# Second block's mixers: block inverses and query rotations held in PSUM, the forget gates' logarithm issued behind the decays

## The chip, the cores and the metric

The kernel runs as one program on one core of a Trainium2 chip. A core has five engines with a queue of instructions each: TensorE (PE in the rows; PEld is its weight load), VectorE (DVE), ScalarE (ACT), GpSimd (POOL) and SyncE (SP), which here only issues DMAs. The metric is device time in microseconds of one execution.

## The reference

Two blocks of two layers each follow one another on one sequence of 256 tokens with 1024 channels, in float32. The change touches the mixers of the second block only. A mixer projects the normalised tokens into four groups, runs one mixer of width 256 on each, and projects the joined results back:

```python
for l in range(DEPTH):                                   # DEPTH = 2
    h = _rms_norm(x, norm1_g[l]) * (1.0 + sc1) + sh1
    pa, pb, pc, pd = _split(h @ w_in[l], GROUP_COLS)
    ya = _rwkv7_mixer(pa, ...)                           # A
    yb = _diff_attn_mixer(pb, ..., cos, sin, lambda_init)  # B
    yc = _spatial_gating_mixer(pc, ...)                  # C
    yd = _forgetting_attn_mixer(pd, ...)                 # D
    y = jnp.concatenate([ya, yb, yc, yd], axis=-1)
    x = x + g1 * (y @ w_out[l])
    h = _rms_norm(x, norm2_g[l]) * (1.0 + sc2) + sh2
    x = x + g2 * _conv_glu_ffn(h, ffn_up[l], ...)
```

Three pieces of it are worked differently after the change:

```python
def step(state, inp):                    # A: a recurrence over the tokens
    sa = einsum('bhvk,bhk->bhv', state, -kk_t)
    state = state * w_t + sa[..., None] * b_t + v_t[..., None] * k_t
    return state, einsum('bhvk,bhk->bhv', state, r_t)

q = _apply_rope(_rms_norm(q, q_g), cos, sin)             # B
k = _apply_rope(_rms_norm(k, k_g), cos, sin)

log_f = jax.nn.log_sigmoid(fl + f_b)                     # D
F = lax.cumsum(log_f, axis=2)
```

The kernel works A's recurrence by blocks of tokens, which needs inverses of triangular 32 x 32 blocks of a matrix of scores.

## The kernel before

The program runs eight stages after one another: GDN mixer, feed-forward, MLA mixer, feed-forward (first block), then mixer, feed-forward, mixer, feed-forward (second block). The second block's mixers lie at about 803 to 985 us and 1205 to 1385 us of the profiled span.

**Weights.** A weight chunk is loaded by SP's queue into `raw`, copied by ACT to a rounded `wh` (L464), and the residue `wl = raw - wh` is made on GpSimd (L467) or VectorE (L469), as a string in the plan says chunk by chunk. Each product takes three matmuls (`wh` with the high and the low part of the tokens, `wl` with the high part): L480 and L483 in one form, L492 to L494 in the other. Three `raw`, `wh` and `wl` buffers rotate.

**Order.** The plan gives the mixer an order string, `B V M b2+L D+S C / e s d c`: after A's scores (`rwkv_scores`) come the pieces of B, A's values (V), the forget gates (M), and so on; a `+` weaves two pieces. A scheduler turns this into one queue for each engine by priority, so an instruction that waits holds up what stands behind it on its engine. PSUM has four banks of tag "acc" for projections, two of tag "mm" and two of tag "A".

**A's scores** (`rwkv_scores`, mixer A). Low-rank inputs `a_P` go through Tanh (L1519, L1520) and a step on VectorE (L1521) to the matmuls `ps_lr` (L1551), which give the decays `a_lw` and the gates `a_av`. Running sums `a_cx` and their exponentials `a_eM`, `a_eK`, `a_eP` (L1571 to L1575) follow, then `a_BD` and `a_bt` on VectorE, and the scores `ps_sc` (L1597). These are copied to `a_UB`, written to DRAM (`dA`), and read back as 32 x 32 blocks into `a_AT` (SBUF, 128 partitions). `tri_inverse` starts from the identity T and makes 31 steps of two VectorE instructions each, a product into `a_stmp` (L1848) and a subtraction from T (L1849). Here T is part of `a_AT`. R, a copy of T, goes through DRAM again to `a_TR`, whose transposes are `ps_tr` (L1705). The first block's GDN mixer calls the same `tri_inverse` with T in a PSUM tile `psT`.

**B's heads** (`diff_heads`). The projection gives queries and keys of 128 tokens in one bank `ps_qk` (tag "acc"), 256 columns each; t = 0 and 1 are the two halves of the tokens. `head_norm` squares (ACT), sums (`hn_s`, VectorE), takes a reciprocal root, and multiplies `ps_qk` into the SBUF tile `b_xn` in one VectorE instruction (L1875), after which the bank is free. The rotation makes six instructions (L1914, L1915) for the queries on VectorE and six for the keys on GpSimd, all from SBUF to SBUF with `b_m` as scratch, into `b_ro`. Four transposes of `b_ro` follow on TensorE (L1925). The next projection, D's, is queued around them on TensorE and takes its banks in turn; `forget_heads` (D) uses `head_norm` too.

**D's gates** (`forget_gates`). With f the gates' input (`flog`, 4 x 256), VectorE makes -|f| (L2045), ACT Exp (L2046) and Ln (L2047) of it, VectorE joins them (L2048) and sums along the tokens (L2051). Exp and Ln need different tables of the scalar engine here, so an ACT_TABLE_LOAD stands ahead of Ln, and one ahead of the Tanh that follows.

The step of the inverse, and the rotation:

```python
V.tensor_tensor(tv, A[:, i, i+1:]..., T[:, i, :m]..., op=ALU.mult)                # L1848
V.tensor_tensor(T[:, i+1:, :m], T[:, i+1:, :m], tv, op=ALU.subtract)              # L1849
```

## Time and profile before

| | us |
|---|---|
| median of 3 runs | 1605.33 (1603.08 to 1606.51) |
| profiled execution | 1601.26 |
| its span | 1599.6 |
| TensorE busy | 1459.0 (91% of the span) |
| VectorE busy | 1148.4 (72%) |
| ScalarE busy | 816.5 (51%) |
| GpSimd busy | 658.3 (41%) |

The profile comes from one execution, 4.07 us below the median of the runs; 1.66 us of it lie outside the span. A share of busy time is an average over eight stages with different limits, so it has to be read stage by stage. A row of a timeline gives start, duration, engine, source line, operation and the tiles with their shapes; in brackets stands the idle time of the engine ahead of it and what ended that. Where a row says x2, x4, ... it joins so many instructions.

### The profile page before, as it was taken

What the parts mean: (1) busy time and instruction counts of PE and PEld (TensorE: products, weight loads), DVE (VectorE), ACT (ScalarE), POOL (GpSimd) and SP (SyncE); (2) the same over time, 40 slices, a digit from 0 to 9 for tenths busy, and PEclk for the clock granted to TensorE, in tenths of its full rate; (3) what the DMA queues carried; (4) which work ended last, traced back from release to release, by engine and by line L of the source; (5) the groups of instructions that cost most, each with busy time, mean ns of one, the idle gap of its engine ahead of it and who ended that gap; (6) DMA issues with size and microseconds to landing.
All of it is one profiled execution on the core that took longest, in us unless ns stands there. A gap on an engine that the chain in (4) does not pass through costs nothing. (4 is left out here: it accounts for less than half of the span.)

```text
span 1599.6 us, 25783 instructions
## 1 busy us (share of the span) xinstructions
PE 1459.0 (91%) x9586; PEld 1289.3 (81%) x9586; DVE 1148.4 (72%) x2348; ACT 816.5 (51%) x1479; POOL 658.3 (41%) x433
## 2 busy tenths in 40 slices
PE   5788989999999899999988889998998788899998
PEld 4788877789988788999877666898887666689987
DVE  4568677678677676997477696788966769676652
ACT  4765545444544564544354465555545446466651
POOL 4455632336443341443136422365534421336630
PEclk9899999999999999999999999999999999899999
DMA  4565531578785455887533324677663332365551
GB/s 161 170 175 173 158 100 57 170 263 305 279 303 184 144 189 187 329 319 298 174 112 116 116 66 134 251 269 265 256 240 127 115 103 67 106 240 184 190 192 40
DMA packets 103247, 292.96 MB, mean 183 GB/s; under 512 B 28073, under 2 KB 37969, under 8 KB 96977
## 3 DMA queue, kind: packets, MB, share of 16 engines
q1 hardware_dynamic: 93872, 237.12, 43.9%
q10 hardware_dynamic: 8896, 53.14, 9.0%
q8 instruction: 75, 1.23, 0.3%
q0 software_dynamic: 352, 1.06, 0.2%
q14 instruction: 52, 0.42, 0.1%
HBM read 288.04 MB, written 3.24 MB: 182 GB/s over the span
## 5 line engine op out<-in xcount | busy, mean ns | idle before, releaser
L467 POOL TENSOR_TENSOR wl<-raw,wh 128x1024 fp32r<-128x1024 f32 (+4 forms) x162 | 395.0, 2445 | 449.8 <-ACT wh L464 378.8
L464 ACT CAST wh<-raw 128x1024 fp32r<-128x1024 f32 (+3 forms) x421 | 422.9, 1018 | 249.6 <-PE ps_o L493 92.3
L469 DVE TENSOR_TENSOR wl<-raw,wh 128x1024 fp32r<-128x1024 f32 (+2 forms) x259 | 346.6, 1348 | 126.7 <-ACT wh L464 122.0
L480 PE MATMUL ps_gu<-h_hi,wh 128*128 128x256 f32 x1280 | 312.9, 283 | 7.3 <-DVE gu_u L2202 7.3
L480 PE MATMUL ps_gu<-h_lo,wh 128*128 128x256 f32 x1280 | 312.4, 283 | 0.0
L480 PEld LDWEIGHTS ps_gu<-h_hi,wh 128*128 128x128 f32 x1280 | 244.6, 191 | 8.2 <-issue 8.0
L480 PEld LDWEIGHTS ps_gu<-h_lo,wh 128*128 128x128 f32 x1280 | 244.7, 191 | 0.2
L1372 DVE CUSTOM_DVE_ANT_0 ada_raw<-ada_raw,ada_cond 128x1024 f32<-128x1024 f32 x96 | 176.2, 1851 | 53.5 <-DMA ada_raw<-in_ada 53.5
L483 PE MATMUL ps_gu<-h_hi,wl 128*128 128x256 f32 x1280 | 178.3, 282 | 4.0 <-POOL wl L467 3.6
L483 PEld LDWEIGHTS ps_gu<-h_hi,wl 128*128 128x128 f32 x1280 | 163.5, 191 | 4.6 <-POOL wl L467 4.0
L494 PE MATMUL ps_o<-wl,act_h 128*128 128x512 f32 x352 | 138.8, 394 | 0.0
L493 PE MATMUL ps_o<-wh,act_l 128*128 128x512 f32 x352 | 138.5, 394 | 0.0
L492 PE MATMUL ps_o<-wh,act_h 128*128 128x512 f32 x352 | 138.4, 393 | 0.0
L2202 DVE SCALAR_TENSOR_TENSOR gu_u<-ps_gu,f2s,gu_u 128x254 f32<-128x254 f32 (+1 forms) x176 | 81.4, 477 | 42.7 <-ACT gu_u L2200 38.8
L725 POOL TENSOR_TENSOR act_l<-gu_t,act_h 128x256 fp32r<-128x256 f32 x44 | 54.0, 1228 | 113.7 <-ACT act_h L724 111.8
L2205 POOL TENSOR_TENSOR gu_t<-gu_t,gu_u 128x256 f32<-128x256 f32 x44 | 49.9, 1134 | 85.0 <-DVE gu_u L2202 82.4
L494 PEld LDWEIGHTS ps_o<-wl,act_h 128*128 128x128 f32 x352 | 66.1, 188 | 15.4 <-issue 0.5
L493 PEld LDWEIGHTS ps_o<-wh,act_l 128*128 128x128 f32 x352 | 66.1, 188 | 15.0 <-issue 0.2
L492 PEld LDWEIGHTS ps_o<-wh,act_h 128*128 128x128 f32 x352 | 66.1, 188 | 15.0 <-issue 0.2
L740 DVE SCALAR_TENSOR_TENSOR cv_y<-ps_g,fi,cv_y 128x253 f32<-128x253 f32 (+2 forms) x96 | 45.0, 478 | 34.8 <-ACT cv_y L738 33.3
L480 PE MATMUL ps_g<-h_hi,wh 128*128 128x256 f32 x256 | 68.4, 300 | 0.0
L2206 ACT CAST act_h<-gu_t 128x256 fp32r<-128x256 f32 x44 | 17.9, 407 | 98.7 <-POOL gu_t L2205 98.5
(653 smaller groups left out, 3031.3 us busy)
## 6 DMA issues: line engine op xcount, KB each, us to landing
ada_raw<-in_ada ACTq DMA_DIRECT2D x48, 1024.0 KB, 5.8
raw<-in_f_gu SPq DMA_DIRECT2D x88, 512.0 KB, 4.5
raw<-in_u_gu SPq DMA_DIRECT2D x88, 512.0 KB, 4.3
raw<-in_f_dn SPq DMA_DIRECT2D x44, 512.0 KB, 4.2
raw<-in_u_dn SPq DMA_DIRECT2D x44, 512.0 KB, 3.7
raw<-in_g_qkv SPq DMA_DIRECT2D x32, 512.0 KB, 3.9
raw<-in_g_z SPq DMA_DIRECT2D x16, 512.0 KB, 4.7
raw<-in_g_out SPq DMA_DIRECT2D x16, 512.0 KB, 3.4
```

The costliest lines, as they stand in the source:

```text
L464: self.last_copy = nc.scalar.copy(wh[:, :cols], raw[:, :cols])
L467: nc.gpsimd.tensor_tensor(wl[:, :cols], raw[:, :cols], wh[:, :cols].bitcast(F32), op=ALU.subtract)
L469: nc.vector.tensor_tensor(wl[:, :cols], raw[:, :cols], wh[:, :cols].bitcast(F32), op=ALU.subtract)
L480: nc.tensor.matmul(ps, wh[:, k * width + m0 : k * width + m0 + m], xx[:, k, :], start=(n == 0), stop=(n == last))
L483: nc.tensor.matmul(ps, wl[:, k * width + m0 : k * width + m0 + m], xh[:, k, :], start=False, stop=(n == last))
L492: nc.tensor.matmul(ps, xh, wh[:, sl], start=start, stop=False, **kw)
L493: nc.tensor.matmul(ps, xl, wh[:, sl], start=False, stop=False, **kw)
L494: nc.tensor.matmul(ps, xh, wl[:, sl], start=False, stop=stop, **kw)
L725: nc.gpsimd.tensor_tensor(al[:, m, :], t, ah[:, m, :].bitcast(F32), op=ALU.subtract)
L1372: nc.vector.tensor_tensor_reduce(raw[:, j], raw[:, j], self.cond, 1.0, 0.0, op0=ALU.mult, op1=ALU.add, accum_out=mod[:, i : i + 1])
L2202: nc.vector.scalar_tensor_tensor(u[:, j, d:], ps[:, j, : S - d], cw[:, 3 * q + 2 - d : 3 * q + 3 - d], u[:, j, d:], op0=ALU.mult, op1=ALU.add)
L2205: nc.gpsimd.tensor_tensor(t, t, u[:, 0], op=ALU.mult)
```

## The change

Three parts, in both mixers of the second block:

- `rwkv_scores`: the matrix T of `tri_inverse` becomes a PSUM tile `ps_ti` of tag "A"; `a_AT` shrinks from 48 to 40 columns of 32. The first operands A and the scratch `a_stmp` stay in SBUF.
- `head_norm` becomes `head_scale`, which ends with the reciprocal root. In `diff_heads` the multiply is made in two halves: the keys from PSUM to `b_xn` (for GpSimd's rotation), the queries in place in `ps_qk`. The query rotation reads `ps_qk` and uses the keys' half of the bank as its scratch, so that each of its instructions has one operand in SBUF. `forget_heads` makes the multiply as before.
- `forget_gates`: Exp and Ln are issued behind the last of the exponentials `a_eP`.

```diff
@@ -1418,7 +1418,7 @@
             gate = self.gate_row(2, mp)
             A = self.rwkv_scores(l, hl, norm, mp, dr)
             B, C, Dd = {}, {}, {}
-            G = dict(B=lambda: self.diff_heads(l, hl, mp, B), C=lambda: self.spatial_in(l, hl, mp, C), D=lambda: self.forget_heads(l, hl, mp, Dd), M=lambda: self.forget_gates(mp, dr, A["f"], Dd),
+            G = dict(B=lambda: self.diff_heads(l, hl, mp, B), C=lambda: self.spatial_in(l, hl, mp, C), D=lambda: self.forget_heads(l, hl, mp, Dd), M=lambda: self.forget_gates(mp, dr, A["f"], Dd, A["last_exp"]),
                      V=lambda: self.rwkv_values(mp, A), L=lambda: self.rwkv_levels(mp, A), S=lambda: self.rwkv_scan(l, mp, A), s=lambda: self.rwkv_out(mp, A, yh, yl),
                      b=lambda: self.diff_attend(l, mp, B), e=lambda: self.diff_out(mp, B, yh, yl), c=lambda: self.spatial_out(l, mp, C, yh, yl), d=lambda: self.forget_attend(l, mp, Dd))
             yh = yl = None
@@ -1572,7 +1572,7 @@
         for m, n in mn:
             nc.scalar.activation(eK[:, m, n], cx[:, m, n, 0:128], AF.Exp, bias=ncm[:, m, n : n + 1])
         for m, n in mn:
-            nc.scalar.activation(eP[:, m, n], cx[:, m, n, 1:], AF.Exp, bias=ncm[:, m, n : n + 1])
+            last_exp = nc.scalar.activation(eP[:, m, n], cx[:, m, n, 1:], AF.Exp, bias=ncm[:, m, n : n + 1])
 
         k2 = t2("k2", [128, 2, S])
         for m in range(2):
@@ -1602,8 +1602,9 @@
             s32 = slice(32 * b, 32 * b + 32)
             nc.sync.dma_start(dA.rearrange("(q b) (j c) -> b j q c", b=4, c=32)[b], UB[s32, :, s32])
 
-        AT = mp.tile([128, 48, 32], F32, name="a_AT", tag="a_z2")
-        A, T, R = AT[:, 0:32], AT[:, 32:40].rearrange("p a b -> p (a b)").rearrange("p (c j) -> p c j", j=8), AT[:, 40:48]
+        AT = mp.tile([128, 40, 32], F32, name="a_AT", tag="a_z2")
+        A, R = AT[:, 0:32], AT[:, 32:40]
+        T = self.pm.tile([128, 32, 8], F32, name="ps_ti", tag="A")
         tmp = mp.tile([128, 256], F32, name="a_stmp", tag="a_y2", bufs=2)
         for g in range(4):
             (nc.sync, nc.scalar)[g % 2].dma_start(A[32 * g : 32 * g + 32].rearrange("p j c -> p (j c)"), dA)
@@ -1614,7 +1615,7 @@
         nc.gpsimd.affine_select(UB, UB, [[0, 8], [1, 128]], ALU.is_ge, 0.0, base=-1, channel_multiplier=-1)
         nc.gpsimd.affine_select(UB, UB, [[0, 8], [1, 128]], ALU.not_equal, 1.0, base=0, channel_multiplier=-1)
         a = locals()
-        a = {n: a[n] for n in "f UB dR BD bt kt k2 eP P7 lora esc kap S0 sel4".split()}
+        a = {n: a[n] for n in "f last_exp UB dR BD bt kt k2 eP P7 lora esc kap S0 sel4".split()}
         a["r"] = project("r", 0)
         a["v"] = project("v", 2)
         return a
@@ -1862,17 +1863,14 @@
             yield
         return ps, pv
 
-    def head_norm(self, mp, dst, ps, nh, hd, eps):
-
-        nc = self.nc
-        V = nc.vector
-        v = ps.rearrange("p (h d) -> p h d", h=nh)
-        nc.scalar.activation(dst, v, AF.Square)
+    def head_scale(self, junk, ps, nh, hd, eps):
+
+        self.nc.scalar.activation(junk, ps.rearrange("p (h d) -> p h d", h=nh), AF.Square)
         ss = self.sm.tile([128, nh], F32, name="hn_s", tag=f"hn_s{nh}")
-        V.tensor_reduce(ss, dst, axis=AX.X, op=ALU.add)
+        self.nc.vector.tensor_reduce(ss, junk, axis=AX.X, op=ALU.add)
         rs = self.sm.tile([128, nh], F32, name="hn_r", tag=f"hn_r{nh}")
         self.rsqrt(rs, ss, (128, nh), 1.0 / hd, eps)
-        V.tensor_tensor(dst, v, rs.unsqueeze(2).to_broadcast([128, nh, hd]), op=ALU.mult)
+        return rs
 
     def diff_heads(self, l, hl, mp, res):
         nc, ap = self.nc, self.ap
@@ -1904,21 +1902,23 @@
             if t == 0:
                 nc.scalar.copy(v, pv)
             xn = mp.tile([128, 16, 32], F32, name="b_xn", tag="b_xn", bufs=2)
-            self.head_norm(mp, xn, ps[t], 16, 32, 1e-6)
-            xv = xn.rearrange("p (q h) (s f) -> p q h s f", q=2, s=2)
+            rs = self.head_scale(xn, ps[t], 16, 32, 1e-6)
+            pv4 = ps[t].rearrange("p (q h d) -> p q h d", q=2, h=8)
+            xn4 = xn.rearrange("p (q h) d -> p q h d", q=2)
+            for q, dst in ((1, xn4[:, 1]), (0, pv4[:, 0])):
+                V.tensor_tensor(dst, pv4[:, q], rs[:, 8 * q : 8 * q + 8].unsqueeze(2).to_broadcast([128, 8, 32]), op=ALU.mult)
             ro = mp.tile([128, 2, 8, 2, 16], F32, name="b_ro", tag="b_ro", bufs=2)
-            m = mp.tile([128, 2, 8, 16], F32, name="b_m", tag="b_m", bufs=1)
+            mk = mp.tile([128, 8, 16], F32, name="b_m", tag="b_m", bufs=1)
+            mq = ps[t][:, 256:384].rearrange("p (h f) -> p h f", h=8)
             tb = lambda i, q: tab[:, t, i, q].unsqueeze(1).to_broadcast([128, 8, 16])
-            for q in range(2):
-                E = nc.gpsimd if q else V
-                mul = lambda o, a, b: (V.tensor_tensor(o, a, b, op=ALU.mult) if not q else nc.gpsimd.tensor_tensor(o, a, b, op=ALU.mult))
-                cmb = lambda o, a, b, op: (V.tensor_tensor(o, a, b, op=op) if not q else nc.gpsimd.tensor_tensor(o, a, b, op=op))
-                mul(ro[:, q, :, 0], xv[:, q, :, 0], tb(0, q))
-                mul(m[:, q], xv[:, q, :, 1], tb(1, q))
-                cmb(ro[:, q, :, 0], ro[:, q, :, 0], m[:, q], ALU.subtract)
-                mul(ro[:, q, :, 1], xv[:, q, :, 1], tb(2, q))
-                mul(m[:, q], xv[:, q, :, 0], tb(3, q))
-                cmb(ro[:, q, :, 1], ro[:, q, :, 1], m[:, q], ALU.add)
+            for q, E, m, xv in ((1, nc.gpsimd, mk, xn4[:, 1]), (0, V, mq, pv4[:, 0])):
+                x1, x2 = (xv[:, :, 16 * i : 16 * i + 16] for i in range(2))
+                E.tensor_tensor(ro[:, q, :, 0], x1, tb(0, q), op=ALU.mult)
+                E.tensor_tensor(m, x2, tb(1, q), op=ALU.mult)
+                E.tensor_tensor(ro[:, q, :, 0], ro[:, q, :, 0], m, op=ALU.subtract)
+                E.tensor_tensor(ro[:, q, :, 1], x2, tb(2, q), op=ALU.mult)
+                E.tensor_tensor(m, x1, tb(3, q), op=ALU.mult)
+                E.tensor_tensor(ro[:, q, :, 1], ro[:, q, :, 1], m, op=ALU.add)
             rf = ro.rearrange("p q h s f -> p (q h s f)")
             pt = self.pm.tile([128, 4, 128], F32, name="ps_qk", tag="mm")
             for j in range(4):
@@ -2020,7 +2020,8 @@
             if t == 0:
                 nc.scalar.copy(v, pv)
             xn = mp.tile([128, 8, 64], F32, name="d_xn", tag="b_xn", bufs=2)
-            self.head_norm(mp, xn, ps[t], 8, 64, 1e-6)
+            rs = self.head_scale(xn, ps[t], 8, 64, 1e-6)
+            V.tensor_tensor(xn, ps[t].rearrange("p (h d) -> p h d", h=8), rs.unsqueeze(2).to_broadcast([128, 8, 64]), op=ALU.mult)
             xf = xn.rearrange("p h d -> p (h d)")
             pt = self.pm.tile([128, 4, 128], F32, name="ps_dq", tag="mm")
             for j in range(4):
@@ -2037,14 +2038,15 @@
             yield
         res.update(v=v, qT=qT, kbd=kbd)
 
-    def forget_gates(self, mp, dr, f, res):
+    def forget_gates(self, mp, dr, f, res, behind):
         nc = self.nc
         V = nc.vector
 
         e = mp.tile([4, S], F32, name="d_e", tag="row", bufs=2)
         V.scalar_tensor_tensor(e, f, -1.0, f, op0=ALU.mult, op1=ALU.min)
-        nc.scalar.activation(e, e, AF.Exp)
-        nc.scalar.activation(e, e, AF.Ln, bias=self.one[0:4], scale=1.0)
+        with self.tc.issue_after(behind.ins):
+            nc.scalar.activation(e, e, AF.Exp)
+            nc.scalar.activation(e, e, AF.Ln, bias=self.one[0:4], scale=1.0)
         V.scalar_tensor_tensor(e, f, 0.0, e, op0=ALU.min, op1=ALU.subtract)
         on = self.one[0:4].to_broadcast([4, S])
         F = mp.tile([4, S], F32, name="d_F", tag="row", bufs=2)
```

How the queues stand before and after. Lines shift by up to two between the versions. The scalar engine at the first mixer's low-rank inputs (`a_P`) before; `d_e` are the forget gates:

```order
L1477 ACTIVATE a_P_8494<-ps_lo,a_om 128x256
L2046 ACTIVATE d_e<-d_e 4x256
L2047 ACT_TABLE_LOAD
L2047 ACTIVATE d_e<-d_e,one 4x256
L1477 ACTIVATE a_k<-ps_k,a_om 128x256
L1519 ACT_TABLE_LOAD
L1519 ACTIVATE a_P_8494<-a_P_8494 32x256
L1520 ACTIVATE a_P_8494<-a_P_8494 64x256
```

The scalar engine after, from the last exponentials `a_eP` to the score copies `a_UB`:

```order
L1575 ACTIVATE a_eP<-a_cx,a_ncm 128x128 x4
L464 CAST wh<-raw 128x768
L2048 ACTIVATE d_e<-d_e 4x256
L464 CAST wh<-raw 128x768
L1477 ACTIVATE a_r<-ps_a,a_om 128x256
L2049 ACT_TABLE_LOAD
L2049 ACTIVATE d_e<-d_e,one 4x256
L1598 COPY a_UB<-ps_sc 128x512
L1477 ACTIVATE a_r<-ps_a,a_om 128x256
L1598 COPY a_UB<-ps_sc 128x512
```

The gates' Exp, table load and Ln moved from ahead of the Tanh to behind the decays, between the shifts `a_r` and ahead of both score copies; the Tanh now has no load ahead of it.

TensorE in the first mixer where D's projection (`ps_qk` and `ps_v` from `wh`, `wl`) meets B's first four transposes, before:

```order
L492 MATMUL ps_v<-wh,h_hi 128x256
L493 MATMUL ps_v<-wh,h_lo 128x256
L492 MATMUL ps_qk<-wh,h_hi 128x512
L493 MATMUL ps_qk<-wh,h_lo 128x512
L494 MATMUL ps_qk<-wl,h_hi 128x512
L492 MATMUL ps_qk<-wh,h_hi 128x512
L493 MATMUL ps_qk<-wh,h_lo 128x512
L494 MATMUL ps_qk<-wl,h_hi 128x512
L492 MATMUL ps_qk<-wh,h_hi 128x512
L493 MATMUL ps_qk<-wh,h_lo 128x512
L1925 MATMUL ps_qk<-ident,b_ro 128x128 x4
L494 MATMUL ps_qk<-wl,h_hi 128x512
```

TensorE at the same place after:

```order
L492 MATMUL ps_qk<-wh,h_hi 128x512
L493 MATMUL ps_qk<-wh,h_lo 128x512
L492 MATMUL ps_v<-wh,h_hi 128x256
L493 MATMUL ps_v<-wh,h_lo 128x256
L1925 MATMUL ps_qk<-ident,b_ro 128x128 x4
L492 MATMUL ps_qk<-wh,h_hi 128x512
L493 MATMUL ps_qk<-wh,h_lo 128x512
L494 MATMUL ps_qk<-wl,h_hi 128x512
L492 MATMUL ps_qk<-wh,h_hi 128x512
L493 MATMUL ps_qk<-wh,h_lo 128x512
L494 MATMUL ps_qk<-wl,h_hi 128x512 x2
L494 MATMUL ps_v<-wl,h_hi 128x256
```

Eight matmuls into the next bank `ps_qk` moved from ahead of the transposes of `b_ro` to behind them.

GpSimd in the first mixer at the key rotations of t = 0 and t = 1 (`b_ro`, `b_m`), before, from the end of the first on:

```order
L1914 TENSOR_TENSOR b_m<-b_xn,b_tab 128x128
L1915 TENSOR_TENSOR b_ro<-b_ro,b_m 128x8x16
L467 TENSOR_TENSOR wl<-raw,wh 128x768 x2
L1914 TENSOR_TENSOR b_ro<-b_xn,b_tab 128x8x16
L1914 TENSOR_TENSOR b_m<-b_xn,b_tab 128x128
```

GpSimd after, from the end of the first rotation to the residues behind the second:

```order
L1920 TENSOR_TENSOR b_m<-b_xn,b_tab 128x128
L1921 TENSOR_TENSOR b_ro<-b_ro,b_m 128x8x16
L1916 TENSOR_TENSOR b_ro<-b_xn,b_tab 128x8x16
L1917 TENSOR_TENSOR b_m<-b_xn,b_tab 128x128
L1919 TENSOR_TENSOR b_ro<-b_xn,b_tab 128x8x16
L1918 TENSOR_TENSOR b_ro<-b_ro,b_m 128x8x16
L1920 TENSOR_TENSOR b_m<-b_xn,b_tab 128x128
L1921 TENSOR_TENSOR b_ro<-b_ro,b_m 128x8x16
L467 TENSOR_TENSOR wl<-raw,wh 128x768 x3
```

The two weight residues that stood between the rotations moved behind the second one, where they join a third.

## Rows read from the trace of the kernel before

**Rows 1.** Stretches: busy us of PE, PEld, DVE, ACT, POOL; granted clock; DMA share; GB/s.

```profile
800.00:960.00 160.00, 133.48 (x791) 109.15 (x790) 125.62 (x429) 82.31 (x182) 63.00 (x59) 0.94 0.32 103
960.00:1200.00 240.00, 224.87 (x1445) 199.00 (x1444) 196.41 (x298) 125.28 (x211) 113.17 (x72) 0.97 0.66 236
1200.00:1360.00 160.00, 135.31 (x793) 110.08 (x792) 119.72 (x402) 81.61 (x178) 54.59 (x54) 0.93 0.33 102
```

**Rows 2.** TensorE's timeline, first mixer: start, duration, what; in brackets the wait.

```profile
832.89 1.22 PE L1551 MATMUL ps_lr<-a_P,a_lora 128*128 128x256 f32 x2 [3.43 <-DVE a_P L1521]
...
847.60 1.97 PE L1597 MATMUL ps_sc<-a_BD,a_bt 128*128 128x256 f32 x8 [1.16 <-DVE a_bt L1585]
...
871.35 0.50 PE L494 MATMUL ps_qk<-wl,h_hi 128*128 128x512 f32 x1 [2.36 <-DVE wl L469]
...
876.72 0.80 PE L492 MATMUL ps_qk<-wh,h_hi 128*128 128x512 f32 x1 [3.46 <-DVE b_xn L1875]
...
883.60 1.12 PE L1925 MATMUL ps_qk<-ident,b_ro 128*128 128x128 f32 x4 [3.28 <-DVE b_ro L1915]
...
891.91 0.66 PE L1925 MATMUL ps_qk<-ident,b_ro 128*128 128x128 f32 x4 [2.27 <-DVE b_ro L1915]
```

**Rows 3.** TensorE's waits, 1225 to 1360: us in total, times, longest.

```profile
PE ps_sc L1597 <- DVE a_bt L1585: 5.3, 1, 5.3
PE ps_qk L492 <- DVE b_xn L1875: 3.5, 1, 3.5
PE ps_qk L1925 <- DVE b_ro L1915: 3.4, 2, 3.0
PE ps_lr L1551 <- DVE a_P L1521: 3.3, 1, 3.3
```

**Rows 4.** Tile a_stmp, 800 to 960: duration min/median/max in ns, first and last start.

```profile
L1848 DVE TENSOR_TENSOR a_stmp<-a_AT x31: 166/216/1757, 860.7 to 895.5; 128x60 f32<-128x60 f32 x3, 128x28 f32<-128x28 f32 x2, 128x54 f32<-128x54 f32 x2, 128x48 f32<-128x48 f32 x2
L1849 DVE TENSOR_TENSOR a_AT<-a_AT,a_stmp x31: 166/218/1890, 862.2 to 895.7; 128x60 f32<-128x60 f32 x3, 128x28 f32<-128x28 f32 x2, 128x54 f32<-128x54 f32 x2, 128x48 f32<-128x48 f32 x2
```

**Rows 5.** The timeline of GpSimd and VectorE, first mixer, residues and operations beside them.

```profile
846.86 2.25 POOL L467 TENSOR_TENSOR wl<-raw,wh 128x768 fp32r<-128x768 f32 x1
847.37 0.47 DVE L1478 SCALAR_TENSOR_TENSOR a_r<-ps_a,lay,a_r 128x255 f32<-128x255 f32 x1
...
863.17 3.65 POOL L467 TENSOR_TENSOR wl<-raw,wh 128x768 fp32r<-128x768 f32 x2 [1.03 <-ACT wh L464]
...
863.19 1.89 DVE L1849 TENSOR_TENSOR a_AT<-a_AT,a_stmp 128x29 f32<-128x29 f32 x1
```

**Rows 6.** VectorE's groups by line, 800 to 960: busy us, mean ns of one, idle before.

```profile
L1849 DVE TENSOR_TENSOR a_AT<-a_AT,a_stmp 128x60 f32<-128x60 f32 (+24 forms) x31 | 10.6, 342 | 0.5
L1848 DVE TENSOR_TENSOR a_stmp<-a_AT 128x60 f32<-128x60 f32 (+24 forms) x31 | 10.1, 324 | 2.9 <-DMA a_AT<-a_dA 2.4
...
L1915 DVE TENSOR_TENSOR b_ro<-b_ro,b_m 128x128 f32<-128x128 f32 x4 | 4.6, 1158 | 0.0
```

**Rows 7.** The same view, 1200 to 1360.

```profile
L1849 DVE TENSOR_TENSOR a_AT<-a_AT,a_stmp 128x60 f32<-128x60 f32 (+24 forms) x31 | 8.8, 284 | 0.4
L1848 DVE TENSOR_TENSOR a_stmp<-a_AT 128x60 f32<-128x60 f32 (+24 forms) x31 | 8.7, 280 | 0.5
```

**Rows 8.** Tile b_xn, 800 to 960, columns as in rows 4.

```profile
L1914 DVE TENSOR_TENSOR b_ro<-b_xn,b_tab x4: 279/414/574, 876.7 to 889.3; 128x128 f32<-128x128 f32 x4
```

**Rows 9.** The timeline of GpSimd and VectorE in the first block.

```profile
136.66 2.38 POOL L467 TENSOR_TENSOR wl<-raw,wh 128x1024 fp32r<-128x1024 f32 x1 [0.31 <-POOL wl L467]
137.23 0.21 DVE L1848 TENSOR_TENSOR stmp<-sA,psT 128x60 f32<-128x60 f32 x1
```

**Rows 10.** ScalarE's timeline, first mixer.

```profile
828.20 1.28 ACT L2047 ACT_TABLE_LOAD   x1
...
830.38 1.28 ACT L1519 ACT_TABLE_LOAD   x1
```

**Rows 11.** One stretch in the first mixer's tail, columns as in rows 1.

```profile
930.00:940.00 10.00, 7.68 (x40) 5.45 (x39) 9.96 (x44) 4.31 (x12) 3.94 (x3) 1.00 0.09 35
```

## Prediction

> **What bounds the kernel now.** I read the busy shares by stage first [rows 1]. In the stretch 960 to 1200 us, which is mostly a feed-forward network, TensorE works 224.87 of 240 us; in the two stretches that hold the second block's mixers it works 133.48 and 135.31 of 160 us, while VectorE works 125.62 and 119.72. So the matmuls bound the feed-forward stages, where the change touches nothing, and in each mixer there are some 25 us in which TensorE waits. Those are what the change can win.
>
> Next I read who ends these waits [rows 2, 3]. In the first mixer TensorE sits 3.43 us before `ps_lr` (low-rank decays, released by `a_P`), 1.16 us before `ps_sc` (scores, released by `a_bt`), and then, in the D projection, 2.36, 3.46, 3.28 and 2.27 us: for a weight residue on VectorE, for the bank that `b_xn` frees, and twice for `b_ro`, the rotated queries. That is 4.6 us ahead of the B projection and 11.4 us behind it. In the second mixer it is 3.3 and 5.3 us ahead, 3.5 and 3.4 us behind. All are ended by VectorE.
>
> Why VectorE is late: its operations with two SBUF inputs stand still while GpSimd runs a tensor_tensor. A step `L1849` on 29 elements takes 1.89 us from 863.19 on, where the median step takes 0.22 [rows 4], and GpSimd's pair of residues runs from 863.17 for 3.65 us [rows 5]. The 62 steps of the inverse take 10.6 + 10.1 us in the first mixer [rows 6] and 8.8 + 8.7 in the second [rows 7]. Sixty-two at 0.217 would be 13.5. So 7.2 and 4.0 us of the inverse are standing still. Of the rotation, the four steps `L1915` take 4.6 us in the first mixer [rows 6] instead of 4 x 0.28 = 1.1, and the eight products 0.42 each instead of 0.28, 1.1 us together (0.28 and 0.41 are the shortest and the median of four of them, [rows 8]). Held time of inverse and rotation: 7.2 + 3.5 + 1.1 = 11.8 us in the first mixer; in the second 4.0 and, by the same products, 1.1, about 5.
>
> **Part 1, the inverse in PSUM.** Each step keeps one SBUF input. Two rows bear on what that is worth. `L1478`, with one input in PSUM, takes 0.47 us in the middle of a 2.25 us residue of GpSimd [rows 5]: not held. And the first block runs this very routine with its matrix in PSUM: a step of 60 elements takes 0.21 us while a 2.38 us residue runs on GpSimd [rows 9], which is the median of the SBUF steps. So I take 0.217 a step and nothing for the hold: -7.2 and -4.0 us of VectorE. The bounds are these and no gain (the hold comes through all the same). The memsets of the matrix, early before, now stand behind the score copy; the inverse waits there for its scores' trip through DRAM, which covers them. `ps_ti` keeps one of the two banks of tag A from the score copies to the copy of R; the next user, `ps_tr`, waits for R's own DRAM trip in any case, so the bank costs nothing.
>
> **Part 2, the query rotation in PSUM.** The normalisation runs over the same 512 columns in two halves, one more start, 0.1 to 0.2 us per tile. The six query steps have one SBUF input each, so -4.6 and -1.1 as above (bounds: these and nothing). The price is in the bank: `ps_qk` of t = 0 was free after one multiply, at 876.7 in the first mixer [rows 2], and is now free after the rotation. In the new order the eight D-projection matmuls that stood before the transposes of t = 0 stand behind them (second pair of fences). They are 883.60 - 3.28 - 876.72 = 3.6 us of TensorE work. I expect the rotation's end well ahead of today's 883.6: of the 11.8 held us some two thirds lie before it (the pair of residues at 863 alone is 3.65, and the two residues that stand between the rotations on GpSimd meet its last step), 8 us, and 3.4 come from part 3 below: about 872. GpSimd's rotation of t = 1 now stands ahead of two residues that stood before it (third pair of fences); the matmuls of these two chunks wait for it, but VectorE's rows for t = 1 end at about that time too, so I count 1 us (bounds 0 and 3, a rotation on GpSimd being six steps of about half a us).
>
> **Part 3, the gates' logarithm.** Before, the scalar engine loads a table for Ln (1.28), runs Ln and a step for `a_k`, and loads a table for Tanh (1.28), all ahead of the Tanh that `a_P` needs [rows 10]. Behind the change the Tanh follows the shift of `a_P` at once; what is left ahead is VectorE: `d_e`'s first step and the `kkn` and `a_k` steps. From 828.20, the first load, to the end of the second, 831.66, is 3.46 us; I take 2.4 for the first mixer, since `a_k` and `kkn` still stand ahead of `a_P` on VectorE, and 0.9 in the second (bounds 0 and 3.46). The first load and Ln are not gone: 830.38 - 828.20 = 2.2 us of it now stand behind the decays, ahead of the score copies, and a load for Exp comes back before B's softmax. TensorE's order also has `ps_sc` further forward, and VectorE's residue moves from ahead of the `a_bt` chain to behind it, so I expect the 1.16 us wait and most of the 5.28 us one to go as well. Taken up to the B projection: -3.4 and -5.0; bounds -4.6 and -8.6 (all waits), and +2.2 (nothing won, and the load delays the score copies).
>
> **The sum.** In the D projection 11.4 us of wait in the first mixer, less the 3.6 us of work that no longer fills the time ahead of t = 0, less 1 for the residues: about -7. In the second VectorE comes 5 us earlier, less 1: -4. With the upstream part -3.4 - 7 = -10.4 and -5 - 4 = -9, together -19.4. Not all of it reaches the end: behind the projections VectorE is busy 9.96 of 10 us at 930 to 940 [rows 11], and the order of VectorE puts D's first head norm of the first mixer, some 5 us of small steps that run in a gap now, behind the copy of R and so into that tail. I give back 3 us there and 1 in the second mixer (bounds 0 and 5 each): -15.4. The feed-forward stages shift as a whole. Profiled execution: 1601.26 - 15.4 = 1585.9; it lies 4.07 under the median of 1605.33, so I say 1590.
>
> **Rivals.**
> *The gain is handed back.* If what VectorE saves is met by work that can't start earlier (R's DRAM trip, the softmax of B behind the projections), each mixer keeps 2 to 3 us: -5, about 1600. For it: the 9.96 of 10 of [rows 11]. Against: the B scores wait for the very rotation that gets faster. 0.12.
>
> *PSUM operands cost more.* 0.217 at the median of 60 elements and 0.28 at 128 make 0.0009 an element, so 255 elements would be 0.40 in SBUF; `L1478` from PSUM takes 0.47 [rows 5]. If that 0.07 is the price of PSUM, some 62 + 14 operations lose 5.3 us in each mixer, half of the first mixer's held time and all of the second's: the gain is about -8, and the time 1597. Against it: the 60-element step of the first block, 0.21 [rows 9]. [...] 0.06.
>
> *The change doesn't do what it says:* VectorE is held in PSUM too, because the one operand left in SBUF is enough. Then only part 3 pays, -8.4, less 3 for the load and the memsets: 1600. Against it stand [rows 5, 9]. 0.05.
>
> *Slower.* The bank `ps_qk` is released by the rotation's last step. Until then TensorE has nothing left, and 3.6 us of matmuls lie behind it. With the rotation at R, they end at R + 3.6, where they ended before the transposes at 883.6 until now: from R = 880 on the mixer loses. With the holds as today, and the Tanh's gain taken back by the load ahead of the score copies, R is 883.6 and each mixer loses 3.6; 7.2 together, some of it hidden by waits that stand there anyway: +6, 1611. 0.07.
>
> **How the numbers follow.** The forecast has 0.70, with its own range 1580 to 1597. Faster by over 0.2% (3.2 us, about what a measurement of this kernel can tell from no change): the forecast, dearer PSUM, two thirds of the first rival and half of the third: 0.70 + 0.06 + 0.08 + 0.03 = 0.87; slower 0.07; same 0.06. For 8 in 10 the range goes up over the handed-back case to 1602, and down to 1578, where nothing is given back and the waits go by 4 us more in each mixer.
>
> **What would show it.** In the profile after: no step of the inverse over 0.3 us, and the group of 62 at 13 to 14 us in each mixer; `b_ro` of t = 0 at least 8 us earlier; the wait for `ps_lr` under 1.5 us in the first mixer; the wait of `ps_qk` for `b_xn` gone, with one for `b_ro` of 3 to 4 us in its place; VectorE over 9.5 of 10 in the tail. The forecast is wrong if single PSUM steps still take over 1 us, if the wait before the transposes of t = 0 is as long as the four waits together are now, or if the waits behind the projections grow by more than 5 us.

## The result, and the profile after

The changed kernel takes 1587.41 us (median of 5 runs, 1584.55 to 1590.53) where the kernel before takes 1603.39 beside it: a ratio of 0.989 with a 95% interval of 0.985 to 0.993. That is 16 us by the medians and 18 by the ratio (12 to 24 by its interval). The forecast was 1590, faster. Run once more beside the last experiments it gave 0.988 (0.986 to 0.991). The profiled execution has a span of 1585.1 us against 1599.6.

Executions of one kernel differ by 10 us and more among themselves (the runs of before range from 1596 to 1613), also in stages that the change doesn't touch: in the profiled execution of after, the first mixer's gate inputs come 5.5 us later than in that of before. So the two traces are compared by marks inside a mixer, each counted from the `flog` instruction (L1516), and only the runs decide what a kernel is worth as a whole. Two of these marks in the trace of after, of VectorE and of TensorE, with start and duration ahead (the second one is the start of the feed-forward stage):

```profile
830.39 0.47 DVE L1516 TENSOR_SCALAR flog<-ps_lo,lay 4x256 f32<-4x256 f32 x1 [2.01 <-PE ps_lo L1513]
```

```profile
991.04 2.05 PE L590 MATMUL ps_t<-ident,xn 128*128 128x128 f32 x16 [0.91 <-DVE xn L582]
```

The mixer lasts 991.0 - 830.4 = 160.6 us by them. (By the same marks the mixers of before end at 994.6 and 1402.4, some 10 and 17 us later than was said ahead of the prediction.) The marks of both kernels, first mixer / second mixer, in us behind `flog`:

| mark | before | after |
|---|---|---|
| `ps_lr` starts | 8.0 / 7.9 | 5.7 / 7.1 |
| `ps_sc` starts | 22.8 / 26.2 | 19.9 / 22.9 |
| the inverse starts | 35.8 / 42.3 | 35.8 / 38.3 |
| transposes of `b_ro`, t = 0 | 58.8 / 61.0 | 51.2 / 51.2 |
| first scores of B, `ps_bs` | 90.7 / 90.6 | 79.8 / 79.4 |
| the feed-forward starts | 169.8 / 177.8 | 160.6 / 165.0 |

The two mixers are 9.2 and 12.8 us shorter in these traces, 22 together, of which the runs confirm 16 to 18.

Now the stretches that answer to [rows 1], columns as there:

```profile
800.00:960.00 160.00, 139.96 (x826) 113.72 (x824) 117.51 (x436) 88.38 (x192) 62.96 (x60) 0.96 0.34 107
...
1200.00:1360.00 160.00, 141.94 (x839) 114.80 (x837) 119.87 (x436) 86.78 (x187) 60.60 (x58) 0.97 0.35 110
```

TensorE works some 6.5 us more in each of them, since a stretch of the same length now holds more of the mixer (826 matmuls instead of 791 in the first). VectorE works 8.1 us less in the first stretch and as much as before in the second. VectorE's groups by line, 800 to 960 (busy us, mean ns of one, idle before), which answer to [rows 6]:

```profile
L1850 DVE TENSOR_TENSOR ps_ti<-ps_ti,a_stmp 128x60 f32<-128x60 f32 (+24 forms) x31 | 6.6, 214 | 0.5
L1849 DVE TENSOR_TENSOR a_stmp<-a_AT,ps_ti 128x60 f32<-128x60 f32 (+24 forms) x31 | 6.3, 202 | 2.7 <-DMA a_AT<-a_dA 2.2
...
L1921 DVE TENSOR_TENSOR b_ro<-b_ro,ps_qk 128x128 f32<-128x128 f32 x2 | 0.6, 288 | 0.0
```

The inverse falls from 20.7 us to 12.9; in the second mixer these two rows read 6.6 and 6.3 as well, from 17.5. No step is over 0.24 us, while GpSimd runs three residues of 5.45 us in all beside them. TensorE's waits in the first mixer, 820 to 960 (in total, times, longest), against [rows 2]:

```profile
PE ps_qk L1925 <- DVE b_ro L1921: 4.2, 1, 4.2
PE ps_sc L1597 <- DVE a_BD L1590: 3.2, 1, 3.2
PE ps_ks L1532 <- ACT a_sq L1529: 2.0, 1, 2.0
...
PE ps_qk L494 <- POOL wl L467: 0.9, 1, 0.9
```

The waits for `a_P` (3.43), for the residue (2.36) and for `b_xn` (3.46) are gone, and of the two for `b_ro` one of 4.2 is left. But the wait for `ps_sc`, which was to go, has grown from 1.16 to 3.2, and one for `a_sq` is new. In the second mixer the same two waits take 4.2 and 3.2 us as well, the latter down from 5.3, and the one for `a_sq` 3.4.

### The profile page after: what moved, and what is told of

The parts are those of the page before. It is cut to its first block, busy times and chain, and to the rows that moved or that the text cites. A ratio compares the mean times of both kernels' runs of the same rounds, so it can differ in the third digit from the quotient of the medians.

```text
span 1585.1 us, 25794 instructions
## 1 busy us (share of the span) xinstructions
PE 1452.5 (92%) x9586; PEld 1285.2 (81%) x9586; DVE 1124.0 (71%) x2352; ACT 817.5 (52%) x1479; POOL 663.6 (42%) x433
## 4 chain that ended last, share of the span: by engine, by line
PE 50%; DVE 17%; DMA 5%; issue 4%; ACT 3%; POOL 2%; SPq 0%; ACTq 0%; DVEq 0%; POOLq 0%
PE ps_gu L480 13%; PE ps_gu L483 6%; PE ps_o L493 6%; PE ps_o L494 6%; PE ps_o L492 6%; DVE wl L469 4%; DVE ada_raw L1372 2%; DMA ada_raw<-in_ada 1%; DVE gu_u L2204 1%; ACT wh L464 1%; DMA raw<-in_u_gu 1%; POOL wl L467 1%; PE ps_u L480 1%; DVE rs_t L519 1%; PE ps_bs L1953 1%
## 5 line engine op out<-in xcount | busy, mean ns | idle before, releaser
L467 POOL TENSOR_TENSOR wl<-raw,wh 128x1024 fp32r<-128x1024 f32 (+4 forms) x162 | 403.6, 2498 | 425.6 <-ACT wh L464 344.3
L493 PEld LDWEIGHTS ps_o<-wh,act_l 128*128 128x128 f32 x352 | 66.1, 188 | 15.1 <-issue 0.2
```

The costliest lines, as they stand in the source:

```text
L467: nc.gpsimd.tensor_tensor(wl[:, :cols], raw[:, :cols], wh[:, :cols].bitcast(F32), op=ALU.subtract)
L493: nc.tensor.matmul(ps, xl, wh[:, sl], start=False, stop=False, **kw)
```

## The experiments

All are compared with the kernel before in the same sitting; a ratio stands with its 95% interval, and us are worked out from it with before at 1604.

### Each part alone

The kernel before with the edit of one part of the diff, nothing else.

> The kernel before with part 1 alone (T of the block inverse in PSUM). Theory H (held time): the 62 steps of the inverse fall to 13 to 13.5 us in both mixers (from 20.7 and 17.5), the rotation keeps its holds, and the time falls by what the inverse sheds ahead of the transposes, about 7 us (4 to 10). Rival O (the new order of the queues carries the gain, since what VectorE saves is met by other waits): the steps get short all the same, but the time falls by 0 to 3 us.

**The inverse alone:** 0.9974 (0.9954 to 0.9994), 4.2 us faster. Its two groups by line in the first mixer, columns as above:

```profile
L1850 DVE TENSOR_TENSOR ps_ti<-ps_ti,a_stmp 128x60 f32<-128x60 f32 (+24 forms) x31 | 6.6, 212 | 0.5
L1849 DVE TENSOR_TENSOR a_stmp<-a_AT,ps_ti 128x60 f32<-128x60 f32 (+24 forms) x31 | 6.2, 200 | 2.8 <-DMA a_AT<-a_dA 2.3
```

The 4.2 us lie inside the 4 to 10 of theory H, but the interval (1 to 7 us) reaches into rival O's range. The hold is gone with part 1 alone. By the marks the transposes of t = 0 come 6.8 and 6.6 us earlier and the first scores of B 10.0 and 6.1; but the feed-forward starts only 0.4 and 5.8 us earlier. This is the rival "handed back", and it is real for this kernel: in the first mixer 9.6 of 10 us are gone again at the feed-forward. Part of that is the mark: 32 matmuls of A (`ps_e`, 6.5 us) stood ahead of B's first scores before and stand behind them here. Over this whole mixer TensorE sits idle 3.8 us less, but its matmuls take 3.4 us longer.

> The kernel before with part 2 alone (query rotation in PSUM, bank of the queries and keys held until its end). Theory H: the rotation sheds 4.6 us of holds in the first mixer and about 1 in the second, and the bank costs up to 3.6 us in each, because the inverse's own holds keep the rotation's end near 880: -3 to +3 us, about 0. Rival O: the order with the eight matmuls behind the transposes is the better one in itself: -4 us or more. The slower mechanism named ahead (the bank) alone would be +4 or more.

**The rotation alone:** 0.9943 (0.9924 to 0.9963), 9.1 us faster, where 0 was expected. The transposes of t = 0 come 1.3 and 4.3 us earlier, at 57.5 and 56.7 behind `flog`, the feed-forward 3.3 and 8.2 us earlier. In the first mixer the rotation ends later than the point (880 - 824.8 = 55.2) from which the slower rival was to decide, and the kernel is still faster. So the bank doesn't have that price. The number falls on rival O's side, but in the changed kernel the old order of the eight matmuls costs nothing (the price of the bank, below), so the order isn't shown to be the reason either. In the second mixer TensorE's idle time is no shorter (28.2 us, 27.5 before): there the gain is in the time that its matmuls take, about 141 us instead of 150, at a mean granted clock of 0.95 instead of 0.91.

> The kernel before with part 3 alone (gates' Exp and Ln behind the decays). Theory H: the wait for the low-rank decays shrinks by 2.4 us in the first mixer and 0.9 in the second, the score matmuls start about 3 us earlier in each, and the time falls by about 6 us (3 to 9). Rival O: the moved order brings the larger part of the whole gain, 8 to 12 us. Third: the trip through DRAM and the load of the table eat it, 0 to 2.

**The gates alone:** 1.0041 (1.0023 to 1.0060), 6.6 us slower. `ps_lr` starts at 5.6 instead of 8.0 in the first mixer, as forecast (in the second it starts 0.6 later), but `ps_sc` only 0.8 and 0.7 earlier and the transposes of t = 0 1.4 us later and 1.1 earlier. What happened to the 2.4 us can be read in the same two groups, first mixer:

```profile
L1848 DVE TENSOR_TENSOR a_stmp<-a_AT 128x60 f32<-128x60 f32 (+24 forms) x31 | 12.0, 386 | 2.6 <-DMA a_AT<-a_dA 2.1
L1849 DVE TENSOR_TENSOR a_AT<-a_AT,a_stmp 128x60 f32<-128x60 f32 (+24 forms) x31 | 10.4, 336 | 0.5
```

22.4 us instead of 20.7: in this mixer work that starts earlier falls under other residues of GpSimd and stands still longer. The four steps of `a_av`, `a_bt` and `a_BD` ahead of the scores take 5.9 us instead of 4.1. In the second mixer neither holds: the inverse takes 17.6 us (17.5 before) and the four steps 5.9 instead of 6.9. The feed-forward starts 4.8 us later in the first mixer and 1.7 earlier in the second, so the added holds account for the first mixer only, and the rest of the 6.6 us isn't explained. In these runs the mean granted clock of TensorE is 0.963, in those of before 0.967.

### Two parts at a time

The changed kernel with one part undone.

> The changed kernel without part 3 (parts 1 and 2). Alone, part 1 brought 4.2 us, part 2 9.1, and part 3 cost 6.6; together they bring about 16 instead of 6.7, so 9 us come from an interplay. Theory C (part 3 always costs its 6.6, and parts 1 and 2 help each other): 22 us below before, 6 faster than the changed kernel. Theory H (part 3's earlier start pays once the inverse and the rotation aren't held): about 13 below before, 3 slower than the changed kernel.

> The changed kernel without part 1 (parts 2 and 3). The singles add up to 2.5 us below before. Theory H (interplay of 3 with the inverse): the inverse keeps its holds, so part 3's earlier start is lost in it: 0 to 4 below before. Rival (interplay of 2 and 3, by the order of the queues): 8 to 12 below before.

> The changed kernel without part 2 (parts 1 and 3). The singles add up to 2.4 us above before. If the interplay is between the inverse and the gates, 5 to 8 us below before; if it is between the inverse and the rotation, within 4 us of before.

| parts | without 3 | with 3 |
|---|---|---|
| neither 1 nor 2 | 1 | 1.0041 |
| 1 | 0.9974 | 0.9921 (0.9901 to 0.9942) |
| 2 | 0.9943 | 0.9975 (0.9958 to 0.9991) |
| 1 and 2 | 0.9894 (0.9871 to 0.9917) | 0.9889, 0.9883 |

Parts 1 and 2 carry the result: 17 us without part 3, against 4.2 + 9.1 = 13.3 taken singly, a difference that the intervals of some 3 us each don't settle. Part 3 adds 1 to 2 us to these two by the runs, which can't be told from nothing; in the traces, one or two for each kernel, the two mixers are 7.5 us shorter with it (325.6 against 333.1). It costs 5 to 7 us where the inverse is held and saves 8.5 where only the inverse is freed. That fits an interplay with the holds, but does not show it: with the rotation freed as well the holds are as much gone, and part 3 saves only 1 to 2. Without part 1 the 4.0 us lie at the edge of theory H's 0 to 4; without part 2 the 12.7 us are more than the 5 to 8 that the interplay with the inverse was to give. Theory C of the first of these runs falls (part 3 isn't a fixed price), and so does H there by its number: 13 was expected, 17 came.

### The price of the bank

The changed kernel, with the queries and their scratch in another bank:

```diff
+            px = self.pm.tile([128, 2, 8, 32], F32, name="ps_xq", tag="mm")
-            for q, dst in ((1, xn4[:, 1]), (0, pv4[:, 0])):
+            for q, dst in ((1, xn4[:, 1]), (0, px[:, 0])):
...
-            mq = ps[t][:, 256:384].rearrange("p (h f) -> p h f", h=8)
+            mq = px[:, 1, :, 0:16]
```

> The changed kernel, with the normalised queries and the scratch of their rotation in a bank of tag mm, so that the projection's bank is free after the two multiplies as it was before the change; the eight matmuls stand ahead of the transposes of t = 0 again. Theory H with a price for the bank: the wait of 4.2 us before the transposes of t = 0 falls by 2 us or more in each mixer and the kernel is 2 to 5 us faster than the changed one (18 to 21 below before). Rival: the bank costs nothing, the work comes later and is hidden: within 1 us of the changed kernel.

0.9903 (0.9888 to 0.9919): 15.6 us below before, so within 3 us of the changed kernel and not faster. The eight matmuls stand ahead of the transposes again; in the first mixer the wait of 4.2 us for `b_ro` is gone, with one of 1.9 for the new bank in its place, as theory H asked, and it gains nothing. The bank, held until the rotation's end, costs nothing that the runs can show; the 3.6 us of the prediction's sum were charged in vain. (They were also read where TensorE's granted clock was low: from 876.72 to 880.10 of before it is 0.51, and six of these eight matmuls take 0.63 us each there, against 0.40 for one at 872.40, where the clock is 1.00.)

### Is it GpSimd that holds VectorE?

The kernel before, with the 768-column residues on VectorE (11 and 6 in the two mixers, 3 in the MLA mixer of the first block) and everything else as it was:

```diff
-        if self.plan["w"][(self.np - 1) % len(self.plan["w"])] == "P":
+        if cols != 768 and self.plan["w"][(self.np - 1) % len(self.plan["w"])] == "P":
```

> The kernel before, its inverse and rotation in SBUF, but with every weight residue of 768 columns (the B and D projections, and three of the MLA mixer) on VectorE instead of GpSimd. Theory of the hold by GpSimd: the 62 steps of the inverse take 13 to 14 us in both mixers with both operands in SBUF, as they do with T in PSUM; VectorE has some 12 us of residues more in each mixer, so the time is 0 to 10 us above before. Rival (SBUF operands themselves are slow in this stage, whoever runs beside them): the steps stay at 17 to 21 us.

0.9914 (0.9880 to 0.9948): 13.8 us faster, 9.6 of it in the two mixers by the marks, though VectorE has more to do (128.50 us busy in 800 to 960 instead of 125.62). Its groups in the first mixer:

```profile
L1849 DVE TENSOR_TENSOR a_AT<-a_AT,a_stmp 128x60 f32<-128x60 f32 (+24 forms) x31 | 7.9, 254 | 0.5
L1848 DVE TENSOR_TENSOR a_stmp<-a_AT 128x60 f32<-128x60 f32 (+24 forms) x31 | 7.2, 233 | 0.3
...
L1914 DVE TENSOR_TENSOR b_ro<-b_xn,b_tab 128x128 f32<-128x128 f32 x4 | 1.7, 414 | 0.0
...
L1915 DVE TENSOR_TENSOR b_ro<-b_ro,b_m 128x128 f32<-128x128 f32 x4 | 1.4, 350 | 0.0
```

15.1 us for the inverse with both operands in SBUF (14.6 in the second mixer), 1 us over what was expected; the four steps L1915 take 1.4 instead of 4.6. The key rotation still runs on GpSimd, and the products L1914 are as held as before (1.7 us). So SBUF operands aren't slow by themselves: the neighbour on GpSimd is the cause. By the runs, most of what the change wins can be had by taking the neighbour away. The forecast of 0 to 10 us slower was wrong: TensorE's idle time falls by 10 us in the two mixers, although VectorE makes each residue itself in about 1 us. How much of that is the hold, and how much residues that are ready sooner, the run doesn't separate.

### Freeing the next held steps

The changed kernel's wait of 3.2 us for `a_BD` is of the same kind. GpSimd and VectorE in its first mixer (start, duration):

```profile
844.64 1.06 POOL L1592 TENSOR_TENSOR a_kap<-a_kkn,a_eK 128x256 f32<-128x256 f32 x1
845.67 1.73 POOL L1586 TENSOR_TENSOR a_kt<-a_k,a_eM 128x512 f32<-128x512 f32 x1
847.35 2.25 POOL L467 TENSOR_TENSOR wl<-raw,wh 128x768 fp32r<-128x768 f32 x1
```

```profile
845.02 1.23 DVE L1590 TENSOR_TENSOR a_BD<-a_kkn,a_eK 64x512 f32<-64x512 f32 x1
846.17 1.76 DVE L1585 TENSOR_TENSOR a_bt<-a_kkn,a_av 128x512 f32<-128x512 f32 x1
847.95 2.20 DVE L1590 TENSOR_TENSOR a_BD<-a_kkn,a_eK 64x512 f32<-64x512 f32 x1
```

Each of the three ends within 0.6 us of an end on GpSimd. The edit keeps the keys in the bank where they are scaled:

```diff
-        V.tensor_tensor(kk, kk, ps, op=ALU.mult)
+        V.tensor_tensor(ps, kk, ps, op=ALU.mult)
+        kp = ps
+        nc.scalar.copy(kk, ps)
...
-        V.tensor_tensor(bt, kk, av, op=ALU.mult)
+        V.tensor_tensor(bt, kp, av, op=ALU.mult)
...
-            V.tensor_tensor(BD[p, :, :, h], split(kk)[p], eK[p], op=ALU.mult)
+            V.tensor_tensor(BD[p, :, :, h], split(kp)[p], eK[p], op=ALU.mult)
```

> The changed kernel, with the normalised keys kept in the PSUM bank of their scaling for a_bt and a_BD (a copy by the scalar engine serves GpSimd). The profile of the changed kernel has TensorE wait 3.2 us in each mixer for a_BD, whose steps of 1.2, 1.8 and 2.2 us lie beside GpSimd's work. Theory of the hold: these steps take about 0.7 us, the score matmuls and the inverse start 2 to 3 us earlier, and the kernel is 2 to 5 us faster than the changed one (18 to 21 below before). Rival: the trip of the scores through DRAM, or the copy on the scalar engine, takes it back: within 1.5 us of the changed kernel.

> The kernel with the normalised keys in PSUM once more: its first profile was of its slowest execution (1588.86, where the median was 1576.6), with mixers only 19.5 us shorter than before. If its times of 1573 to 1584 hold, it is 20 to 30 us below before, and a profile near them shows the mixers about 25 us shorter, with the score matmuls 4 us or more earlier in both. If the low times were chance, it is 16 to 20 below, like the changed kernel.

0.9835 (0.9807 to 0.9864), and once more 0.9853 (0.9822 to 0.9883): 1576.6 and 1580.65 us in the median, 24 to 26 us below before and faster than both kernels. VectorE and TensorE in the second mixer of the repeat: the steps in PSUM, and the two longest waits and the one for the scores:

```profile
1237.47 0.69 DVE L1587 TENSOR_TENSOR a_bt<-ps_kb,a_av 128x512 f32<-128x512 f32 x1
1238.07 1.38 DVE L1592 TENSOR_TENSOR a_BD<-ps_kb,a_eK 64x512 f32<-64x512 f32 x2
```

```profile
PE ps_qk L1927 <- DVE b_ro L1923: 4.3, 1, 4.3
PE ps_ks L1532 <- ACT a_sq L1529: 3.4, 1, 3.4
PE ps_sc L1599 <- DVE a_BD L1592: 1.0, 1, 1.0
```

They take 0.69 us each, and the wait for `a_BD` falls from 3.2 to 1.0; `a_av` ahead of them, with both operands still in SBUF, takes 2.18 us there. `ps_sc` starts at 19.0 and 22.0 behind `flog`, the inverse at 33.0 and 36.8 (35.8 and 38.3 in the changed kernel); the mixers last 159.6 and 164.8. So the repeat shows 23.2 us in the mixers, where 25 was expected, and the scores 3.8 and 4.2 us earlier than before, where 4 or more was; that is only about 1 us earlier than in the changed kernel. Its mixers are no more than 1.2 us shorter than the changed kernel's, while its runs are some 6 us faster: where the rest of that lies isn't shown.

> Parts 1 and 2 and the normalised keys in PSUM, without part 3. If part 3 gains where the chain that it starts earlier isn't held by GpSimd's residues (a_bt, a_BD in PSUM, then the inverse), this kernel is 3 us or more slower than the one with the keys in PSUM and all three parts (26 us below before): 20 to 23 below before. If part 3 pays nothing in any company, it is within 2 us of that one.

Without part 3, the keys in PSUM bring 0.9902 (0.9874 to 0.9929), 15.7 us: no more than parts 1 and 2 alone. With part 3 it is 24 to 26. That is the theory's side and more than its 3 us: by the runs part 3 is worth its place beside the keys. That this is because the chain is no longer held is argued, not shown: the traces place only 4 of the 8 to 10 us in the mixers, all in the first, and in the second the inverse starts no earlier with part 3 (36.8 us behind `flog`, 36.4 without). The mixers without it are 19.3 us shorter than before, inside the interval of its runs (11 to 20); TensorE's mean granted clock is 0.967 in these runs and 0.973 in those with part 3.

> The changed kernel once more, beside the other two: 14 to 20 us below before (17.8 by the ratio of its first runs), mixers from the gates' input to the next feed-forward about 22 us shorter in all.

It gave 18.8 us below before, the mixers 159.6 and 165.9, 22.1 us shorter.

## Why the prediction was right, point by point

**The hold, its size and its cure: right.** The 62 steps were put at 13 to 14 us and take 12.9 in both mixers; the twelve query steps take 3.4 us in each mixer, as eight products and four sums at 0.28 to 0.30 each, from 8.0 and 4.8. The runs show the cause as well: with the residues off GpSimd most of it goes without any PSUM (15.1 us in the first mixer, from 20.7). The normalisation in two halves takes 0.41 to 0.43 us a half, where the whole took 0.67 to 0.68: about 0.15 more a tile, where 0.1 to 0.2 was put.

**PSUM operands dearer: falls.** A rotation step of 128 columns takes 0.28 to 0.30 with PSUM, 0.28 was the shortest in SBUF [rows 8]; the inverse's 12.9 us are under the 13.5 that 0.217 a step gave. So neither is longer than the SBUF rows gave, and the 0.07 an operation that the rival took from `L1478` doesn't show in them.

**TensorE's waits in the projection: right.** One wait for `b_ro` of 4.2 us (3 to 4 forecast) and 0.85 for a residue behind GpSimd's rotation (1 forecast; its six steps take 0.45 to 0.47 each) stand for 11.4 in the first mixer, with one of 0.96 for `at_v` that is new. In the second mixer the list of the prediction left out 2.4 us for residues on VectorE; 4.2 us for `b_ro` stand there now.

**Up to the inverse: the step that failed.** The sum had -3.4 and -5.0 from part 3. `ps_lr` is earlier by 2.3 and 0.8, as forecast. `ps_sc` is earlier by 2.9 and 3.3. But the inverse starts 0.0 and 4.0 earlier. Two terms were missed. The wait for `ps_sc` didn't go: the earlier chain ran into GpSimd's products and a residue, and `a_BD` and `a_bt` with their neighbour `a_av` take 5.9 us instead of 4.1 in the first mixer (rows under "Freeing the next held steps"); in the second they take 5.9 instead of 6.9, and the wait falls from 5.3 to 3.2. And the scores' trip through DRAM, which I took as fixed, grew from 13.0 to 15.9 us in the first mixer (16.1 and 15.4 in the second). The DMA queues in the trace of before, then of after, with a step of ACT:

```profile
850.21 1.83 SPq L1603 DMA_DIRECT2D a_dA<-a_UB  x4
...
854.00 0.81 ACTq L1609 DMA_DIRECT2D a_AT<-a_dA  x2
```

```profile
853.39 1.82 SPq L1603 DMA_DIRECT2D a_dA<-a_UB  x4
...
859.76 0.83 ACT L464 CAST wh<-raw 128x768 fp32r<-128x768 f32 x1 [1.31 <-PE ps_v L493]
859.92 0.81 ACTq L1610 DMA_DIRECT2D a_AT<-a_dA  x2
```

The loads of the blocks are issued from the scalar engine's queue 2.0 us behind the last store before, 4.7 after: they now stand behind a weight cast that waits for a matmul of the projection until 859.8. So `b_ro` of t = 0 is 7.6 us earlier in the first mixer and not the 12 of the sum, just under the 8 named as a sign; in the second it is 9.8.

**Part 3: mis-sized.** It had -8.4 us of the sum. On top of parts 1 and 2 it brings 1 to 2 (the table of the parts), and alone it costs 6.6. What I weighed as a small loss, the load ahead of the score copies, wasn't the reason: the copies wait 3.2 us for `ps_sc` with the load long done. The reason seen, in the first mixer, is that the chain that it frees is itself held; in the second it isn't held longer, and there the cause stays open.

**Parts 1 and 2: mis-sized the other way.** They had -11 by the waits, less the give-back, and bring 17. The 3.6 us for the bank and 4 us of give-back weren't taken in the changed kernel: from the first scores of B to the feed-forward it takes 80.8 and 85.6 us, before 79.1 and 87.2, although 443 matmuls instead of 391 stand there in the first mixer. VectorE works 9.25 and 9.75 of 10 us there, where over 9.5 was forecast (stretches of after, columns as in rows 1):

```profile
922.00:932.00 10.00, 10.00 (x71) 7.85 (x71) 9.25 (x57) 7.46 (x21) 0.00 (x0) 1.00 0.00 1
932.00:942.00 10.00, 10.00 (x66) 8.01 (x64) 9.75 (x37) 5.69 (x14) 2.65 (x2) 1.00 0.22 61
```

but TensorE works through both stretches.

**TensorE's clock: a term that the sum didn't have.** The prediction took the waits as all that the change could win. From `flog` to the feed-forward both kernels make the same 827 matmuls in each mixer (before, then after, columns as in rows 1):

```profile
824.84:994.61 169.77, 145.30 (x827) 113.94 (x825) 129.09 (x435) 89.76 (x206) 67.65 (x59) 0.94 0.32 102
1224.65:1402.40 177.75, 150.22 (x827) 116.65 (x826) 136.01 (x439) 90.86 (x206) 58.83 (x54) 0.91 0.32 101
```

```profile
830.39:991.04 160.65, 140.90 (x827) 110.77 (x825) 117.66 (x441) 90.89 (x206) 66.00 (x59) 0.97 0.35 109
1223.29:1388.24 164.95, 144.06 (x827) 112.55 (x825) 125.90 (x446) 90.63 (x206) 58.99 (x54) 0.96 0.35 109
```

Of the 22 us, 11.4 are idle time of TensorE (24.5 and 27.5 us before, 19.8 and 20.9 after), where the sum had 19.4 before its give-back. The other 10.6 are the matmuls' own time, 295.5 us before and 285.0 after; in the second trace of the changed kernel the two are 13.4 and 8.6. What goes with it is the granted clock, in the last column but two: 0.94 and 0.91 before, 0.97 and 0.96 after. Read by half microseconds from 830 to 925 of before, it is 1.00 in 160 of the 190 and 0.50 in 25. The four transposes of [rows 2] take 1.12 us at 883.60, behind a wait of 3.28 us, and 0.66 at 891.91:

```profile
883.60:884.72 1.12, 1.12 (x5) 0.74 (x5) 1.12 (x4) 0.00 (x0) 0.00 (x0) 0.50 0.45 181
891.91:892.57 0.66, 0.66 (x6) 0.66 (x7) 0.66 (x2) 0.00 (x0) 0.00 (x0) 1.00 0.00 0
```

The runs bear it out: the mean granted clock is 0.967 over 59 of before and 0.972 over 11 of the changed kernel. That the shorter waits brought the higher clock is not shown. With the residues on VectorE the idle time falls by 10 us as well, and the clock of the mixers stays at 0.94 and 0.90 and the matmuls' time at 296 us. So the forecast of 1590 came out partly by luck: part 3 brought far less than its term, parts 1 and 2 brought more, and half of the gain is of a kind that the prediction didn't count.

**What stays open.** The stretch behind the projections differs between these kernels by up to 11 us (78 to 89 us in the first mixer). It doesn't hold the same work (391 to 443 matmuls, as the orders of the queues change with each edit), and the clock differs too. With one or two traces for each kernel I can't say which order is the good one. D's first head norm alone doesn't decide it: it stood behind the copy of R before the change already (907.9 and 895.9 us) and moved from 83 to 93 us behind `flog`; in the kernel with the bank freed early it comes at 73, and that takes 84.7 us.

## What to carry to other kernels

Where a small VectorE step takes 1.5 to 2 us in one place and 0.2 in the next, look at what GpSimd runs at that moment before looking at the step: here one operand in PSUM (the inverse in 12.9 us, from 20.7), or the neighbour on another engine (15.1), took most or all of the hold away. A wait that was cut ahead of a chain brought nothing here while the chain itself was held, so try to free the chain first, and then start it earlier. Measure the parts of a change alone and in pairs: here one of three slows the kernel by itself, brings nothing with two others, and 8 to 10 us by the runs beside a fourth edit, which frees steps behind it. And read the matmuls' own time and the granted clock beside TensorE's waits: here they held half of the gain in the traces.

## What the runs showed that I had not expected

GpSimd's residue of 768 columns takes 1.8 us, and the six held steps of the inverse beside it in the trace of before 1.54 to 1.89, where the median step takes 0.22. Done by VectorE itself the same residue takes about 0.95 us. So with VectorE held, GpSimd's help cost more than it gave here: moving these residues to VectorE made the kernel 13.8 us faster without another edit.
